# Fourier branch: the position sums made once for both mirrored halves, z gated by one Silu, and a gate group placed first of the eight projection groups

## The chip, the cores and the metric

One Trainium2 chip, one core of it. The metric is the device time of one execution in microseconds (us). It was 1290.96 us before, the median of 3 runs (1290.1 to 1291.08). Everything is float32; each product is made of three matmuls of rounded parts, as shown below.

## The reference, cut to what matters

```python
def _fourier_mix(u):                       # u: (1, 512, 512), four channel groups of 128
    ug = u.reshape(b, n, 4, 128)
    y = jnp.fft.fftn(ug, axes=(1, 3), norm="ortho").real
    return y.reshape(b, n, 512)

def _merge(p_rest, attn, w_pa, w_pb, w_o): # p_rest: columns of h @ w_in
    ...
    g_a = sigmoid(...); g_b = sigmoid(...)                 # 2 x 2048 gate columns
    y_a = (attn * silu(z_a)) @ w_pa
    y_b = (_fourier_mix(u_b) * silu(z_b)) @ w_pb
    return (g_a * y_a + g_b * y_b) @ w_o

# h = modulate(rmsnorm(x)), p = h @ w_in;  q (12 heads) and k are normalised per head and rotated (rope);
# hc = modulate(rmsnorm(ctx)) gives 256 more keys and values;  out = rmsnorm(x + gate * y)
```

512 tokens, 256 context tokens, width 2048, `w_in` has 9216 columns. The transform of a group is 512 points over the tokens by 128 over the channels. With A the transform over the tokens, the result at token frequency k is C·Re A(k) plus or minus S·Im A(k), where C and S are the cosine and sine tables over the 128 channels, and frequency 512-k has the same two sums with the other sign.

## The kernel before, in words

**Three matmuls for one product.** A float32 operand is split in a rounded part "hi" (ScalarE, ACT, L180) and the rest "lo" (VectorE, DVE, L181). A product is hi·hi + hi·lo + lo·hi, three matmuls on TensorE (PE, L338, L339, L340, the function `mm3`). Weights stream from HBM, are split in the same way, and each split buffer is given back when PE has used it, so ACT and DVE run some five pieces ahead of PE and no further.

**The start** (0 to 144 us) makes h and, from the first weight columns, u and z of the Fourier branch. z stands in `part[:, 4:8]`.

**The channel stage** (144.6 to 156.1 us) is the Fourier transform, for channel groups g of 0 to 3. `tokens(g)` makes the transform over the tokens, frequencies 0 to 256, in two accumulators (even and odd frequencies), and splits them into `ah` and `al`. `positions(g)` makes the sums over the channels: before, it makes 512 outputs in one accumulator `pd`, the columns 0 to 255 and the columns 256 to 511 from the mirrored frequencies (a slice with step -1), each with its own matmuls; `fch` holds the split tables cos, -sin and sin. One DVE instruction (L944) scales the result and multiplies it with the gated z. `gate_b(g)` gates z: Sigmoid on ACT (L949) and a product on DVE (L950). PE's order in this stage is written out by hand: tokens 0, tokens 1, positions 0, tokens 2, positions 1, tokens 3, positions 2, positions 3.

**Eight projection groups** (156.1 to about 810 us) follow, each 1024 columns of `w_in` by a fast product of seven block products, `P1, Q5, P2, Q6, P7, Q3, Q4`, four pieces of weights each. A piece is 12 matmuls of 512 columns, so a group has 28 pieces. `KINDS` names what a group yields: "qz" (512 columns of q and 512 of z_a), "gate" (1024 gate columns), "kv". In the first group (g == 0) DVE also makes and splits the sums of h's blocks that all groups use (`make_form`, `split_form`, L993, L994). A group's results come in four blocks: (0,0) after P2, (1,1) after P7, (0,1) after Q3, (1,0) after Q4.

- A gate block: one Sigmoid (L1182) and a store by ACT's DMA queue (L1183).
- A qz block (0,0) or (1,0) is rotated by `rotated`: squares on ACT (L1208), products into the tile `qr` and into a PSUM scratch pair (DVE, L1210 and L1212), the root on GpSimd (POOL, L1196, L1197), the add (L1215) and the scaling (L1216) on DVE, then two stores of 256 KB each from `qr` on ACT's DMA queue (L1230). A block of z_a takes Tanh and one product.
- PSUM pairs with the tag "y" take turns in two slots: Q5's accumulator, the scratch of a rotation and that of a Tanh.

**The context** needs its own norm. `context_squares` (four pieces `cn`) sums squares, `context_norm` makes the root and two diagonal blocks (DVE, L1315) in the first 256 columns of `qr`, `context_spread` spreads the norms over the partitions by two matmuls on PE (L1320), and `context_row` (four pieces `cr`) writes the modulated context into `qr` and stores it to `cf_d`, from where the kv group reads it. `context_piece` sets beside which piece of which group they stand. `qr` is thus shared by the rotations and the context.

**Order.** After the channel stage a scheduler orders the instructions of each engine when the program is built; on the chip each engine runs its list in that order and waits where an operand is late. `jobs` are small steps, one taken behind each piece.

Of the kernel before, what the change touches and what calls it, by code (L numbers as in the profile page):

```python
# [10 lines left out]
F32 = mybir.dt.float32  # L11
F32R = mybir.dt.float32r
# [6 lines left out]
P = 128  # L19
D = 2048  # L20
T = 512
# [26 lines left out]
EVEN = 258  # L48
# [16 lines left out]
KINDS = ("qz", "qz", "qz", "gate", "gate", "kv", "gate", "gate")  # L65
# [57 lines left out]
def block_kernel(ctx, tc, xT, ctx_rows, ctx_toks, x, c_row, w_ss, w_gate, vecs, qkg, rope, dft_c, dft_s,  # L123
# [243 lines left out]
    for p in start_pieces():  # L367
        if p[2:5:2] == (KK - 4, 0):
            stream(("dfts", 0), dft_s[:, : 2 * EVEN], 2 * EVEN, 2, "raw")
            stream(("dftc", 0), dft_c, 3 * P, 1, "raw")  # L370
        elif p[2:5:2] == (KK - 4, 4):
            stream(("dfts", 1), dft_s[:, 2 * EVEN :], T, 2, "raw")
        stream(("start", p), w_start[p[0] : p[0] + P * p[1]].rearrange("(p c) -> p c", p=P), p[1], p[2 + 1])
# [146 lines left out]
    fch = ppool.tile([P, 2, 3 * P], F32R, name="fch")  # L520
    fsq = [ppool.tile([P, 2, 2, EVEN], F32R, name="fsq0")]
# [374 lines left out]
    fsq.append(fnp.tile([P, 2, 2, 256], F32R, name="fsq1"))  # L896
# [21 lines left out]
    def tokens(g):  # L918

        ah, al = (fnp.tile([P, 2, 257], F32R, tag=n, bufs=2, name=uid(n)) for n in ("ah", "al"))  # L920
        c = slice(P * g, P * g + P)
        for e in range(2):
            n = fsq[e].shape[-1]
            acc = bank()
            for a in range(2):
                mm3(acc[:, :n], uh[:, a, e, c], ul[:, a, e, c], fsq[e][:, 0, a, :], fsq[e][:, 1, a, :], a == 0, a == 1)
            k = slice(e, 257 - e, 2)
            low[g] = split_from(acc[:, :n].rearrange("p (r f) -> p r f", r=2), ah[:, :, k], al[:, :, k])[1]
        AH[g] = ah, al

    def positions(g):

        ah, al = AH.pop(g)
        acc = bank2()
        steps = [(256 * q, P * (r and 1 + q), (slice(0, 256) if q == 0 else slice(256, 0, -1)), r)
                 for q in range(2) for r in range(2)]
        for n, (o, t, k, r) in enumerate(steps):
            for m, i in enumerate((0, 1)):
                nc.tensor.matmul(acc[:, o : o + 256], fch[:, i, t : t + P], ah[:, r, k], start=n == m == 0, stop=False,
                                 skip_group_check=True)  # L940
        for n, (o, t, k, r) in enumerate(steps):
            nc.tensor.matmul(acc[:, o : o + 256], fch[:, 0, t : t + P], al[:, r, k], start=False, stop=n == 3,
                             skip_group_check=True)
        nc.vector.scalar_tensor_tensor(part[:, 4 + g, :], acc, 1.0 / 256.0, part[:, 4 + g, :], op0=ALU.mult, op1=ALU.mult)  # L944

    def gate_b(g):
        z = part[:, 4 + g, :]
        e = fnp.tile([P, T], F32, tag="sil", bufs=1, name=uid("e"))
        nc.scalar.activation(e, z, ACT.Sigmoid)  # L949
        nc.vector.tensor_tensor(z, z, e, op=ALU.mult)  # L950
# [269 lines left out]
    def qz_done(half, c, v, t):  # L1220

        if c:
            e = pair("x" if half else "y")
            nc.scalar.activation(e, v, ACT.Tanh, scale=0.5)
            nc.vector.scalar_tensor_tensor(v, e, 1.0, v, op0=ALU.add, op1=ALU.mult)
            r = v.rearrange("p t (h d) -> p t h d", h=4)
        else:
            r = rotated(half, v, pair("y"))
        for b in range(2):
            nc.scalar.dma_start(qz_d[4 * group.g : 4 * group.g + 4, :, c, 2 * half + b, :].rearrange("h p d -> p h d"),  # L1230
                                r[:, b])
# [72 lines left out]
    def context_squares(i, raw):  # L1304

        nc.scalar.activation(raw, raw, ACT.Square, accum_out=sums[:, i : i + 1])

    def context_norm():

        ss = sums[:, 4:6]  # L1310
        nc.vector.tensor_tensor(ss, sums[:, 0:4:2], sums[:, 1:4:2], op=ALU.add)
# [11 lines left out]
    def context_row(i, raw):  # L1323
# [11 lines left out]
        for j in range(2):  # L1335
            sa, sb = (shift[:, 2 * i + j + 8 * q, 1:2] for q in range(2))
            d = sums[:, 6 + j : 7 + j]
# [651 lines left out]
def _constants():  # L1989
# [10 lines left out]
    dft_c = np.concatenate([np.cos(a), -np.sin(a), np.sin(a)], axis=1).astype(np.float32)  # L2000
# [6 lines left out]
    dft_s = np.concatenate([table(np.arange(0, T // 2 + 1, 2)), table(np.arange(1, T // 2, 2))], axis=1)  # L2007
# [3 lines left out]
def _layout(x, c, ctx, c_ctx, w_ada, b_ada, norm_g, w_in, q_norm_g, k_norm_g, w_proj_a, w_proj_b, w_out, final_g):  # L2011
# [36 lines left out]
    d["w_g"] = blocks(np.concatenate(heads + [w_in[:, O_GA:O_GB], w_in[:, O_K:O_ZA], w_in[:, O_GB:]], axis=1))  # L2048
# [20 lines left out]
```

## Time and profile before

| | |
|---|---|
| time, median of 3 runs | 1290.96 us |
| the profiled execution's own time | 1290.61 us |
| its span (first to last instruction) | 1288.8 us |
| granted TensorE clock | 0.998 |
| PE busy | 1272.9 us, 99% of the span |
| DVE busy | 994.7 us, 77% |
| ACT busy | 682.2 us, 53% |
| POOL busy | 170.8 us, 13% |
| read from HBM | 283.36 MB |

Matmuls are pipelined: a matmul of 512 columns is shown with about 390 ns, but the next starts 227 ns after it. Time lost on PE is read from the distance of starts, not from the busy share. Starts and durations are in us from the span's start. "T" below is the start of a projection group on PE. Numbers behind tile names (whi, wlo, wr, s, y, x, pd) are buffer numbers of the build and mean nothing else.

### The profile page before, as it was taken

What the parts mean: (1) busy time and instruction counts of PE and PEld (TensorE: products, weight loads), DVE (VectorE), ACT (ScalarE), POOL (GpSimd) and SP (SyncE); (2) the same over time, 40 slices, a digit from 0 to 9 for tenths busy, and PEclk for the clock granted to TensorE, in tenths of its full rate; (3) what the DMA queues carried; (4) which work ended last, traced back from release to release, by engine and by line L of the source; (5) the groups of instructions that cost most, each with busy time, mean ns of one, the idle gap of its engine ahead of it and who ended that gap; (6) DMA issues with size and microseconds to landing.
All of it is one profiled execution on the core that took longest, in us unless ns stands there. A gap on an engine that the chain in (4) does not pass through costs nothing.

```text
span 1288.8 us, 17680 instructions
## 1 busy us (share of the span) xinstructions
PE 1272.9 (99%) x6586; PEld 1047.9 (81%) x6586; DVE 994.7 (77%) x1305; ACT 682.2 (53%) x1073; POOL 170.8 (13%) x222
## 2 busy tenths in 40 slices
PE   8999999999999999999999999999999999999997
PEld 5677887888888888888888888888888888888886
DVE  5767899889779787658587666788898777887677
ACT  5322654645556555444355544666667646464544
POOL 0000011111102011012031010012100211211210
PEclk9999999999999999999999999999999999999999
DMA  9998588888988988977879897578852989998986
GB/s 378 408 369 344 208 216 248 237 218 261 227 302 236 301 269 260 291 197 184 278 207 259 286 249 237 182 245 241 270 178 75 249 244 258 244 211 229 225 200 179
DMA packets 104486, 319.14 MB, mean 248 GB/s; under 512 B 9904, under 2 KB 33072, under 8 KB 100432
## 3 DMA queue, kind: packets, MB, share of 16 engines
q1 hardware_dynamic: 55056, 197.40, 42.3%
q0 software_dynamic: 27024, 98.19, 35.6%
q10 hardware_dynamic: 22320, 22.42, 5.1%
q8 instruction: 51, 0.84, 0.3%
q14 instruction: 35, 0.29, 0.1%
HBM read 283.36 MB, written 34.61 MB: 247 GB/s over the span
## 4 chain that ended last, share of the span: by engine, by line
PE 91%; DVE 3%; DMA 2%; ACT 2%; issue 1%; SPq 0%; ACTq 0%; DVEq 0%
PE banks L338 10%; PE banks L339 10%; PE banks L340 10%; PE x L340 9%; PE x L338 9%; PE x L339 9%; PE y L340 7%; PE y L339 7%; PE y L338 7%; PE banks L1543 2%; PE pd L566 2%; PE pb L338 1%; PE pb L339 1%; PE pb L340 1%; PE pc L338 1%; DMA wa<-in_w_ss 1%
## 5 line engine op out<-in xcount | busy, mean ns | idle before, releaser
L180 ACT ACTIVATE whi<-R 128x1024 fp32r<-128x1024 f32 x138 | 145.6, 1060 | 142.1 <-PE banks L340 55.3
L181 DVE TENSOR_TENSOR wlo<-R,whi 128x1024 fp32r<-128x1024 f32 x138 | 167.9, 1222 | 57.9 <-ACT whi L180 57.6
L181 DVE TENSOR_TENSOR wlo<-wr,whi 128x1024 fp32r<-128x1024 f32 (+1 forms) x122 | 147.2, 1214 | 63.1 <-ACT whi L180 63.1
L180 ACT ACTIVATE whi<-wr 128x1024 fp32r<-128x1024 f32 (+1 forms) x122 | 127.4, 1052 | 127.3 <-PE y L340 44.3
L338 PE MATMUL banks<-whi,s 128*128 128x512 f32 (+1 forms) x400 | 157.8, 394 | 0.9 <-DVE ev L1106 0.9
L339 PE MATMUL banks<-wlo,s 128*128 128x512 f32 (+1 forms) x400 | 155.8, 389 | 0.0
L340 PE MATMUL banks<-whi,s 128*128 128x512 f32 (+1 forms) x400 | 155.8, 389 | 0.0
L338 PE MATMUL x<-whi,s 128*128 128x512 f32 x352 | 137.1, 390 | 0.0
L340 PE MATMUL x<-whi,s 128*128 128x512 f32 x352 | 137.0, 389 | 0.0
L339 PE MATMUL x<-wlo,s 128*128 128x512 f32 x352 | 136.9, 389 | 0.0
L338 PE MATMUL y<-whi,s 128*128 128x512 f32 x316 | 123.1, 389 | 0.2 <-DVE cxe L1266 0.2
L339 PE MATMUL y<-wlo,s 128*128 128x512 f32 x316 | 123.1, 390 | 0.0
L340 PE MATMUL y<-whi,s 128*128 128x512 f32 x316 | 122.8, 389 | 0.0
L291 POOL DMA_DIRECT2D R<-in_w_g x64 | 56.0, 875 | 415.2 <-DVE wlo L181 212.6
L180 ACT ACTIVATE s<-wr 128x512 fp32r<-128x512 f32 (+2 forms) x93 | 60.9, 678 | 68.1 <-DMA wr<-cf_d 24.9
L338 PEld LDWEIGHTS banks<-whi,s 128*128 128x128 f32 x400 | 75.2, 188 | 16.6 <-DVE ev L1106 1.3
L181 DVE TENSOR_TENSOR s<-wr,s 128x512 fp32r<-128x512 f32 (+2 forms) x93 | 66.7, 750 | 28.3 <-ACT s L180 27.5
L340 PEld LDWEIGHTS banks<-whi,s 128*128 128x128 f32 x400 | 75.1, 188 | 15.3
L339 PEld LDWEIGHTS banks<-wlo,s 128*128 128x128 f32 x400 | 75.2, 188 | 13.6 <-DVE wlo L181 0.2
L340 PEld LDWEIGHTS x<-whi,s 128*128 128x128 f32 x352 | 66.1, 188 | 13.8
L339 PEld LDWEIGHTS x<-wlo,s 128*128 128x128 f32 x352 | 66.1, 188 | 13.7
L338 PEld LDWEIGHTS x<-whi,s 128*128 128x128 f32 x352 | 66.1, 188 | 13.6
(322 smaller groups left out, 2803.2 us busy)
## 6 DMA issues: line engine op xcount, KB each, us to landing
wr<-in_w_g SPq DMA_DIRECT2D x128, 512.0 KB, 5.8
R<-in_w_g POOLq DMA_DIRECT2D x64, 512.0 KB, 7.3
wa<-in_w_ss SPq DMA_DIRECT2D x31, 1024.0 KB, 9.7
R<-in_w_g SPq DMA_DIRECT2D x32, 512.0 KB, 6.0
wr<-in_w_gate SPq DMA_DIRECT2D x32, 512.0 KB, 5.1
wr<-in_w_o SPq DMA_DIRECT2D x24, 512.0 KB, 7.5
R<-in_w_o POOLq DMA_DIRECT2D x24, 512.0 KB, 9.2
wr<-in_w_pab SPq DMA_DIRECT2D x20, 512.0 KB, 6.0
```

The source lines that it names most:

```text
L180: first = nc.scalar.activation(hi, src, ACT.Copy)
L181: return first, nc.vector.tensor_tensor(lo, src, hi.bitcast(F32), op=ALU.subtract)
L291: nc.gpsimd.dma_start(chain[e.pc], e.nxt, accum_op=ALU.add)
L338: nc.tensor.matmul(o, ah, bh, start=start, stop=False, skip_group_check=cont)
L339: nc.tensor.matmul(o, ah, bl, start=False, stop=False, skip_group_check=cont)
L340: nc.tensor.matmul(o, al, bh, start=False, stop=stop, skip_group_check=cont)
L566: nc.tensor.matmul(acc[32 * j : 32 * j + 32], c2[:, n, :], w[:, k, :], start=n < 4, stop=n >= KK - 4)
L1543: nc.tensor.transpose(tp[:, k * P : (k + 1) * P], p[:, k * P : (k + 1) * P], ident)
```

## The change

What it does:

- `positions` makes two sums of 258 columns, C·Re A in the accumulator `pd` and S·Im A in `pc`, by three matmuls each. ACT copies the second to SBUF (`odd`), DVE subtracts (columns 0 to 256) and adds in mirrored order (columns 257 to 511) and multiplies with z. The table of sines loses its second copy, the scale 1/256 goes into the table, and the odd frequencies get one more (257), so that both halves have 258 columns.
- `gate_b` is one Silu on ACT, in place.
- `KINDS` starts with a gate group, the three qz groups come second to fourth, and the columns of `w_g` are laid out to match. The context's squares, norm and rows move with them: squares in the fourth group from P7 on, the norm behind the first piece of the fifth group, the spread two jobs later, and the rows at pieces 5, 10, 15 and 20 of the fifth group.

```diff
-KINDS = ("qz", "qz", "qz", "gate", "gate", "kv", "gate", "gate")
+KINDS = ("gate", "qz", "qz", "qz", "gate", "kv", "gate", "gate")
...
+CTX_NORM, CTX_ROWS = (16, 18, 20, 22), (33, 38, 43, 48)
 def context_piece(g, name, pc):
     n = 28 * (g - NQZ) + 4 * ONE_GROUP.index(name) + pc
-    if n % 2 == 0 and 0 <= n < 8:
-        return "cn", n // 2
-    if n % 7 == 4 and 18 <= n < 46:
-        return "cr", n // 7 - 2
+    if n in CTX_NORM:
+        return "cn", CTX_NORM.index(n)
+    if n in CTX_ROWS:
+        return "cr", CTX_ROWS.index(n)
...
     def tokens(g):
-        ah, al = (fnp.tile([P, 2, 257], F32R, tag=n, bufs=2, name=uid(n)) for n in ("ah", "al"))
+        ah, al = (fnp.tile([P, 2, FREQ], F32R, tag=n, bufs=2, name=uid(n)) for n in ("ah", "al"))
...
     def positions(g):
         ah, al = AH.pop(g)
-        acc = bank2()
-        steps = [(256 * q, P * (r and 1 + q), (slice(0, 256) if q == 0 else slice(256, 0, -1)), r)
-                 for q in range(2) for r in range(2)]
-        for n, (o, t, k, r) in enumerate(steps):
-            for m, i in enumerate((0, 1)):
-                nc.tensor.matmul(acc[:, o : o + 256], fch[:, i, t : t + P], ah[:, r, k], start=n == m == 0, stop=False,
-                                 skip_group_check=True)
-        for n, (o, t, k, r) in enumerate(steps):
-            nc.tensor.matmul(acc[:, o : o + 256], fch[:, 0, t : t + P], al[:, r, k], start=False, stop=n == 3,
-                             skip_group_check=True)
-        nc.vector.scalar_tensor_tensor(part[:, 4 + g, :], acc, 1.0 / 256.0, part[:, 4 + g, :], op0=ALU.mult, op1=ALU.mult)
+        acc = [b()[:, :FREQ] for b in (bank2, bank3)]
+        for r, o in enumerate(acc):
+            t = slice(P * r, P * r + P)
+            mm3(o, fch[:, 0, t], fch[:, 1, t], ah[:, r, :], al[:, r, :], True, True)
+        z = part[:, 4 + g, :]
+        y, odd = (fnp.tile([P, n], F32, tag=t, bufs=2, name=uid(t)) for t, n in (("y", T), ("odd", FREQ)))
+        nc.scalar.copy(odd, acc[1])
+        nc.vector.tensor_tensor(y[:, :257], acc[0][:, :257], odd[:, :257], op=ALU.subtract)
+        nc.vector.tensor_tensor(y[:, 257:], acc[0][:, 255:0:-1], odd[:, 255:0:-1], op=ALU.add)
+        nc.vector.tensor_tensor(z, y, z, op=ALU.mult)

     def gate_b(g):
         z = part[:, 4 + g, :]
-        e = fnp.tile([P, T], F32, tag="sil", bufs=1, name=uid("e"))
-        nc.scalar.activation(e, z, ACT.Sigmoid)
-        nc.vector.tensor_tensor(z, z, e, op=ALU.mult)
+        nc.scalar.activation(z, z, ACT.Silu)
...
     def context_norm():
-        ss = sums[:, 4:6]
+        ss = sums[:, 28:30]
...
     for g, kind in enumerate(KINDS):
-        if g == 3:
-            jobs += [lambda: None] * 12 + [context_norm, lambda: None, lambda: None, context_spread]
+        if g == KV - 1:
+            jobs += [context_norm, lambda: None, context_spread]
...
-    dft_c = np.concatenate([np.cos(a), -np.sin(a), np.sin(a)], axis=1).astype(np.float32)
+    dft_c = (np.concatenate([np.cos(a), np.sin(a)], axis=1) / 256.0).astype(np.float32)
...
-    dft_s = np.concatenate([table(np.arange(0, T // 2 + 1, 2)), table(np.arange(1, T // 2, 2))], axis=1)
+    dft_s = np.concatenate([table(np.arange(e, FREQ, 2)) for e in range(2)], axis=1)
```

The line numbers of the changed kernel are other ones: what is L268, L276, L1106, L1210, L1212, L1215, L1216, L1315, L1320 before is L271, L279, L1105, L1209, L1211, L1214, L1215, L1314, L1319 after.

**PE, channel stage, before:** `positions(0)` and the first product of `tokens(2)`.

```order
L939 MATMUL pd252_1482<-ah243_1439,fch_146 128x256 x8
L942 MATMUL pd252_1482<-al244_1440,fch_146 128x256 x4
L338 MATMUL pb255_1498<-fsq0_147,uh_1346 128x258
L339 MATMUL pb255_1498<-fsq0_147,uh_1346 128x258
L340 MATMUL pb255_1498<-fsq0_147,ul_1347 128x258
```

**PE, the same place, after:**

```order
L341 MATMUL pd251_1480<-ah243_1439,fch_146 128x258
L342 MATMUL pd251_1480<-al244_1440,fch_146 128x258
L343 MATMUL pd251_1480<-ah243_1439,fch_146 128x258
L341 MATMUL pc252_1481<-ah243_1439,fch_146 128x258
L342 MATMUL pc252_1481<-al244_1440,fch_146 128x258
L343 MATMUL pc252_1481<-ah243_1439,fch_146 128x258
L341 MATMUL pb257_1496<-fsq0_147,uh_1346 128x258
```

Twelve matmuls became six, and the first one that reads `al` stands second, where it stood ninth.

**DVE, end of the channel stage, before,** from the last `al` of `tokens(2)` on (`al260` is that of `tokens(3)`).

```order
L181 TENSOR_TENSOR al254_1497<-pb256_1507,ah253_1496 128x2x128
L181 TENSOR_TENSOR wlo268_1575<-R1_1340,whi267_1574 128x1024
L944 SCALAR_TENSOR_TENSOR part_108<-pd258_1519,part_108 128x512
L181 TENSOR_TENSOR al260_1534<-pb261_1535,ah259_1533 128x2x129
L181 TENSOR_TENSOR al260_1534<-pb262_1544,ah259_1533 128x2x128
L181 TENSOR_TENSOR wlo272_1596<-R2_1341,whi271_1595 128x1024
L944 SCALAR_TENSOR_TENSOR part_108<-pd266_1560,part_108 128x512
```

**DVE, the same place, after** (`al264` is that of `tokens(3)`).

```order
L184 TENSOR_TENSOR al256_1495<-pb258_1505,ah255_1494 128x258
L943 TENSOR_TENSOR y261_1523<-pd259_1515,odd262_1524 128x257
L944 TENSOR_TENSOR y261_1523<-pd259_1515,odd262_1524 128x255
L184 TENSOR_TENSOR al264_1530<-pb265_1531,ah263_1529 128x258
L945 TENSOR_TENSOR part_108<-y261_1523,part_108 128x512
L184 TENSOR_TENSOR al264_1530<-pb266_1540,ah263_1529 128x258
L943 TENSOR_TENSOR y271_1562<-pd269_1554,odd272_1563 128x257
L944 TENSOR_TENSOR y271_1562<-pd269_1554,odd272_1563 128x255
L184 TENSOR_TENSOR wlo274_1569<-R1_1340,whi273_1568 128x1024
```

Three DVE rows stand where L944 stood, and the split of the second weight piece (`wlo` from R1) moved behind the last `al`.

**DVE, the diagonal blocks of the context's norm, before** (fourth group, a gate group, among the splits for P7).

```order
L276 TENSOR_TENSOR wr504_3569<-R0_1339,wr504_3569 128x1024
L181 TENSOR_TENSOR s72_434<-R3_1342,s70_433 128x2x256
L1315 TENSOR_SCALAR qr_1617<-ident_86,small_97 128x128 x2
L181 TENSOR_TENSOR s97_572<-wr504_3569,s95_571 128x2x256
L276 TENSOR_TENSOR wr507_3587<-R1_1340,wr507_3587 128x1024
```

**DVE, the same instruction, after** (fifth group, during P1, right behind the last rotation of the fourth group).

```order
L1211 TENSOR_TENSOR y549_3894<-ev504_3488,qr_1609 128x8x32 x2
L184 TENSOR_TENSOR s72_434<-R3_1342,s70_433 128x2x256
L1214 TENSOR_TENSOR qr_1609<-qr_1609,y549_3894 128x1024
L184 TENSOR_TENSOR s97_572<-wr562_4014,s95_571 128x2x256
L1215 TENSOR_TENSOR qr_1609<-qr_1609,small_97 128x1024
L184 TENSOR_TENSOR s128_735<-wr562_4014,s126_734 128x2x256
L1314 TENSOR_SCALAR qr_1609<-ident_86,small_97 128x128 x2
L184 TENSOR_TENSOR wlo566_4061<-wr563_4034,whi565_4060 128x1024
```

The blocks are now written into `qr` one row behind the scaling (L1215), whose result the two stores of 256 KB have to read out of `qr` first.

**PE, the spread of the context's norm, after:** in the second piece of Q5 of the fifth group, 69 matmuls behind the group's start (48 of P1, 21 of Q5).

```order
L341 MATMUL y559_3995<-whi555_3960,s287_1658 128x512
L342 MATMUL y559_3995<-wlo556_3961,s287_1658 128x512
L343 MATMUL y559_3995<-whi555_3960,s288_1659 128x512
L1319 MATMUL y557_3977<-qr_1609,ones_91 128x128 x2
L341 MATMUL y559_3995<-whi555_3960,s287_1658 128x512
```

Before, the same two matmuls stood at the end of Q6 of the fourth group. The accumulator y559 of this Q5 lies in the PSUM slot that held y549, the scratch of the last rotation.

More of the change, by code (lines that the diff above doesn't have):

```diff
@@ L47 @@
 HL, MORE_HL = 3, 2
-EVEN = 258
+FREQ = 258
 FORMS = ("Z5", "S2", "S3", "S4")
@@ L1229, in qz_done @@
         for b in range(2):
-            nc.scalar.dma_start(qz_d[4 * group.g : 4 * group.g + 4, :, c, 2 * half + b, :].rearrange("h p d -> p h d"),
+            nc.scalar.dma_start(qz_d[4 * group.g - 4 : 4 * group.g, :, c, 2 * half + b, :].rearrange("h p d -> p h d"),
                                 r[:, b])
```

30 lines of the change are left out of this document (15 added, 15 removed).

## Prediction, on record before the changed kernel ran

> **What bounds the kernel now.** The first part of the page says it:
>
> ```profile
> PE 1272.9 (99%) x6586; PEld 1047.9 (81%) x6586; DVE 994.7 (77%) x1305; ACT 682.2 (53%) x1073; POOL 170.8 (13%) x222
> PE 91%; DVE 3%; DMA 2%; ACT 2%; issue 1%; SPq 0%; ACTq 0%; DVEq 0%
> ```
>
> The second row, from the chain that ended last, shows that PE is the path nearly everywhere. So a matmul taken away counts in full, and work added to DVE, ACT or a queue counts only where PE then waits for it. Next the windows, one row for the channel stage and one for each of the first five projection groups (length, then PE, PEld, DVE busy):
>
> ```profile
> 144.60:156.10 11.50, 11.50 (x97) 11.50 (x96) 11.22 (x21) 8.48 (x16) 0.53 (x1) 1.00 0.20 79
> 156.10:234.10 78.00, 77.05 (x339) 62.89 (x338) 75.57 (x88) 42.22 (x63) 10.51 (x13) 1.00 0.80 229
> 234.10:310.20 76.10, 76.10 (x337) 63.04 (x336) 66.77 (x80) 40.99 (x77) 11.33 (x12) 1.00 0.89 249
> 310.20:386.40 76.20, 76.20 (x337) 63.07 (x337) 59.41 (x75) 41.80 (x81) 10.76 (x12) 1.00 0.87 251
> 463.00:539.20 76.20, 76.20 (x337) 63.07 (x337) 55.85 (x78) 39.49 (x51) 6.90 (x8) 1.00 0.90 274
> ```
>
> A group costs 76.2 us when PE never waits; the first costs 78.0, with DVE busy 75.6 of them. PE's timeline shows where most of the 1.8 us goes, each time at a form or weight that DVE has split late:
>
> ```profile
> 208.06 0.39 PE L338 MATMUL x<-s,s 128*128 128x512 f32 x1
> 209.16 0.50 PE L339 MATMUL x<-s,s 128*128 128x512 f32 x1 [0.71 <-DVE s L181]
> 212.01 0.39 PE L339 MATMUL y<-s,s 128*128 128x512 f32 x1
> 212.64 0.50 PE L340 MATMUL y<-s,s 128*128 128x512 f32 x1 [0.24 <-DVE s L181]
> ```
>
> Starts 1.10 and 0.63 apart instead of 0.23 (as 386.40 to 386.63 below): 1.3 us lost, plus restarts.
>
> **The channel stage.** Positions before, on PE:
>
> ```profile
> 154.68 1.12 PE L939 MATMUL pd<-ah,fch 128*128 128x256 f32 x8
> 155.64 0.65 PE L942 MATMUL pd<-al,fch 128*128 128x256 f32 x4
> 156.13 0.40 PE L338 MATMUL x<-whi,s 128*128 128x512 f32 x1
> ```
>
> Twelve matmuls from 154.68 to 156.13 are 1.44 us, 0.120 each. The change takes 24 of 48 away: 24 x 0.120 = 2.9 us. The two columns more in each matmul are under 0.1 us together.
>
> What they covered is tight, though. The first matmul on `al` was the ninth, now it is the second. The durations are these:
>
> ```profile
> L180 ACT ACTIVATE ah<-pb x8: 392/409/419, 145.5 to 153.4; 128x258 fp32r<-128x258 f32 x4, 128x256 fp32r<-128x256 f32 x4
> L181 DVE TENSOR_TENSOR al<-pb,ah x8: 417/422/428, 146.4 to 153.9; 128x258 fp32r<-128x258 f32 x4, 128x256 fp32r<-128x256 f32 x4
> 155.36 0.69 DVE L944 SCALAR_TENSOR_TENSOR part<-pd,part 128x512 f32<-128x512 f32 x1
> 145.80 0.69 DVE L950 TENSOR_TENSOR part<-part,e 128x512 f32<-128x512 f32 x1
> 138.43 1.28 ACT L949 ACT_TABLE_LOAD   x1
> ```
>
> Followed through the new order from 144.6 on, tokens 3 ends on PE at 151.8 and positions 3 starts at 152.5. DVE, which has no idle time here, reaches the last `al` at about 153.2 and ends it at 153.5, while PE wants it at 152.6. So about 0.9 us of the gain is given back; the ends are 0 (DVE on time) and 1.4 (one DVE row of 512 later). DVE's own work hardly changes: four L944 and four L950 go (4.8 us at 0.6 from start to start), four rows each of 257, 255 and 512 columns come (5.1 us). No row shows a mirrored read on DVE; L1212 reads swapped halves of 256 columns at 0.43, like `al`, so I take that, with nothing and 0.34 more for each as ends. The `odd` copies are 0.4 each on ACT, idle for 3 of 11.5 us here. Silu has no row; I take Sigmoid's, and nothing on the path follows from it for some 5 us. The gate group first costs one more table load, 1.28 us on ACT, idle for 36 us in that group: nothing. Net of the stage: -2.0 us.
>
> **The first group.** As a gate group it loses the first rotation's DVE rows that stood before 208 us:
>
> ```profile
> L1210 DVE TENSOR_TENSOR qr<-x,qr x8: 683/688/692, 193.6 to 592.6; 128x512 f32<-128x512 f32 x8
> L1212 DVE TENSOR_TENSOR y<-x,qr x12: 422/427/433, 194.2 to 353.9; 128x256 f32<-128x256 f32 x12
> L1216 DVE TENSOR_TENSOR qr<-qr,small x8: 1217/1220/1226, 202.7 to 670.0; 128x1024 f32<-128x1024 f32 x8
> ```
>
> Two L1210, four L1212, an L1215 and an L1216: by starts 2 x 0.6 + 4 x 0.33 + 2 x 1.13 = 4.8 us. PE arrives 2.0 earlier and had waited 1.8, together 3.8; DVE is 4.8 - 1.3 (the new waits inside the channel stage) = 3.5 earlier. It nearly breaks even: I let 0.4 us of waits stay, so -1.4 us. Ends: -1.8 and 0.
>
> **The context's norm behind the last rotation.** This is new, and PE waits for it. The fourth group is now a qz group; its last rotation falls into P1 of the fifth. Two things hang on it: Q5 takes the PSUM slot of the rotation's scratch, free when the add (L1215 before) ends; and the spread's diagonal blocks go into `qr`, free when the first store of the rotation has landed. Where these stood for the three qz groups before, with the start of the next group on PE first:
>
> ```profile
> 234.08 0.39 PE L338 MATMUL x<-whi,s 128*128 128x512 f32 x1
> 246.50 1.22 DVE L1215 TENSOR_TENSOR qr<-qr,y 128x1024 f32<-128x1024 f32 x1
> L1230 ACTq DMA_DIRECT2D qz_d<-qr x2: 366/692/1017, 249.1 to 249.5; - x2
> DMA to landing us min/median/max: 4.7/5.5/6.3
> ...
> 310.24 0.39 PE L338 MATMUL x<-whi,s 128*128 128x512 f32 x1
> 319.54 1.22 DVE L1215 TENSOR_TENSOR qr<-qr,y 128x1024 f32<-128x1024 f32 x1
> L1230 ACTq DMA_DIRECT2D qz_d<-qr x2: 366/443/520, 323.1 to 323.5; - x2
> DMA to landing us min/median/max: 8.6/8.8/9.0
> ...
> 386.40 0.39 PE L338 MATMUL x<-s 128*128 128x512 f32 x1
> 386.63 0.39 PE L339 MATMUL x<-s,s 128*128 128x512 f32 x1
> 400.07 1.22 DVE L1215 TENSOR_TENSOR qr<-qr,y 128x1024 f32<-128x1024 f32 x1
> L1230 ACTq DMA_DIRECT2D qz_d<-qr x2: 367/528/688, 403.6 to 404.0; - x2
> DMA to landing us min/median/max: 11.8/13.1/14.3
> ```
>
> The add ends at T+13.6, T+10.4 and T+14.8, the first store is issued at T+15.0, T+12.9 and T+17.2 and lands (the "min") 4.7, 8.6 and 11.8 us later. None of this cost anything, because nobody needed `qr` or the slot soon. Now PE does: Q5 starts at T + 48 x 0.2267 = T+10.9, the spread at T + 69 x 0.2267 = T+15.65.
>
> By the new order, with these durations: DVE takes the subtraction of (1,0) at about T+1.6, and the splits between the rotation's rows have to wait for weight buffers that PE frees a piece at a time; the third piece's, at T+8.2, sets the last squares on ACT (end T+9.8) and the last L1212 (T+10.5). The add ends at T+12.3, POOL's root too (2.3 us), the scaling at T+14.0. Q5 waits 1.4 us (0 to 3.9 by the three rows). The store is issued at T+14.0. Three or four other transfers are under way then, as in the first two cases, so I take 6 us to land, between 4.7 and 8.6. The blocks take 0.6 more: the spread at T+20.6, 5.0 us late in all, Q5's wait included. Ends: 1.4 (see the quick store below) and 14 (third case: 17.2 + 11.8 + 0.6 - 15.65). DVE is stopped behind the same store, but pieces up to the first of P2 are split ahead, 9 us of PE's work, so nothing is added.
>
> The row that shows the opposite is the store of a rotation in mid-group:
>
> ```profile
> DMA to landing us min/median/max: 2.4/2.6/2.8
> ```
>
> [...]
>
> **The rest.** The context's rows add DVE work of about 8 us to the fifth group, which has 20 idle. The kv group's read of `cf_d` now comes some 25 us later, near the group's start; ends 0 and 4 us, I take 0.
>
> **Sum**, against the profiled execution (span 1288.8, its own time 1290.61, which is 0.35 below the median): -2.0 - 1.4 + 5.0 = +1.6 us. On the median: 1290.96 + 1.6 = 1292.6 us. 0.2%, 2.6 us, is what a measurement of this kernel can tell from no change; this is inside.
>
> **Rivals.**
> - *The store lands late* (the other side): as in the second and third case, 8.6 to 11.8 us, PE stands at the spread until T+23 to T+30, 7.5 to 14 us late: +4 to +10.6, 1295 to 1301.5. It decides from a landing of 7 us on. For it: two of three rows. Against: DVE, stopped at the blocks, frees no raw buffers, so fewer loads can follow the store. 0.28.
> - *The store lands in its quick time,* 2.4 to 2.6 us: the spread would be ready at T+17.0, which Q5's wait of 1.4 covers: -2.0, 1289. [...] Against: all three rows at a group's start. 0.14.
> - *No wait there at all:* the rotation ends earlier (the fourth group has DVE to spare, and T+10.4 was seen once), and the first group gains all: -2.9 to -4.7, 1286.3 to 1288.1. 0.17.
> - *The first group's waits stay* because PE's lead of 2 us meets a DVE that is as late as before: +1.4 on the forecast, 1294. 0.04.
>
> **How the numbers follow.** Forecast, landing 3.5 to 7 us, 1290 to 1293.6: 0.37. Faster: the third rival, with a little of the quick store, 0.19. Same: forecast and most of the quick store, 0.47. Slower: the first and the last rival and the forecast's edge, 0.34. The range for 8 in 10 leaves out half of the third rival and the late end of the first: 1287.5 to 1299.
>
> **What would show it.** Right: 24 matmuls in `pd` and `pc`; a PE wait of about 1 us for `al` before positions 3; the first group at 76.2 to 77; the fifth at 80 to 83, with a wait before Q5's first matmul and one before L1319, the blocks (L1314) held by the store. Wrong: the fifth group at 76.6 or below (no wait), or above 84 (late landing); the first group still at 78; a kv group over what it had.

## The result, and the profile after

The changed kernel took 1300.58 us (median of 5 runs, 1299.31 to 1301.76) against 1290.96; the ratio is 1.0076, with a 95% interval of 1.0062 to 1.009. The forecast was 1292.6, its range up to 1299.0. The profiled execution took 1299.31 us, 1.3 below its median, with a span of 1297.5: 8.7 more than before.

First the page's busy times, then the windows of the stage, the first, fourth and fifth group and the kv group (which has 504 matmuls of 512 columns, where the others have 336), and of before's fourth and kv group for comparison (length, then PE, PEld, DVE, ACT, POOL busy, clock, DMA share, GB/s):

```profile
PE 1271.7 (98%) x6562; PEld 1045.4 (81%) x6562; DVE 996.0 (77%) x1308; ACT 685.2 (53%) x1077; POOL 167.6 (13%) x222
```

```profile
144.60:155.00 10.40, 9.14 (x74) 8.74 (x72) 9.07 (x20) 7.02 (x17) 0.53 (x1) 1.00 0.11 41
155.00:232.20 77.20, 76.80 (x337) 63.02 (x338) 73.48 (x85) 43.78 (x51) 8.57 (x11) 1.00 0.81 242
384.50:460.70 76.20, 76.20 (x338) 63.12 (x337) 62.32 (x75) 44.55 (x84) 12.34 (x14) 1.00 0.86 253
460.70:545.30 84.60, 78.98 (x341) 64.39 (x340) 62.52 (x103) 43.09 (x72) 8.90 (x10) 0.98 0.80 237
545.30:661.40 116.10, 114.75 (x505) 94.38 (x504) 80.20 (x91) 44.20 (x71) 10.61 (x13) 1.00 0.83 251
```

```profile
386.40:463.00 76.60, 76.60 (x341) 63.50 (x340) 65.24 (x93) 43.44 (x72) 11.65 (x12) 1.00 0.91 273
539.20:654.00 114.80, 114.59 (x505) 94.48 (x504) 76.59 (x87) 43.12 (x68) 10.62 (x13) 1.00 0.80 226
```

The stage is 1.1 us shorter (11.5 before), the first group 0.8 (78.0), the fourth 0.5 (76.6: the spread of the context's norm stood there); up to the fifth group the changed kernel is 2.4 us ahead. The fifth group is 8.5 longer, and 0.5 of that is the spread itself, which it now has. In the kv group PE is idle for 1.35 us, where it was for 0.2. Something is lost later too: PE's waits, longest first, from 144 us to the end (the second figure is how often; a wait counts from the modelled end of the matmul ahead, so the loss from start to start is 0.1 to 0.2 more):

```profile
PE y L1319 <- DVE qr L1314: 3.8, 1, 3.8
PE y L342 <- DVE wlo L184: 1.7, 2, 1.3
PE y L341 <- ACT ev L1267: 1.3, 1, 1.3
PE banks L341 <- DVE ev L1105: 0.9, 1, 0.9
PE pd L342 <- DVE al L184: 0.8, 1, 0.8
PE banks L1656 <- DMA s<-yb_d: 0.7, 1, 0.7
PE y L341 <- DVE qr L1214: 0.5, 1, 0.5
PE banks L341 <- DVE R L1490: 0.5, 1, 0.5
PE x L341 <- ACT odd L942: 0.5, 1, 0.5
```

L1105 (0.9) stood before too. New are the two of the channel stage (al, odd), one at 172 us in the first group (the smaller L184, 0.4), four in the fifth group and the kv group (L1214, L1314, the longer L184, L1267), and two late ones (R L1490 at 909 us, s<-yb_d at 1131). In sum: stage -1.1, first group -0.8, fourth -0.5, fifth +8.5, kv +1.25, seventh and eighth -0.2, the rest +1.5, together the 8.7. The medians differ by 9.6; the profiled execution is the fastest of the five, and what the others lose more is on no trace.

**The fifth group** starts on PE at T = 460.65. The rotation's last rows on DVE, its store on ACT's queue with the time to landing, and PE at the spread:

```profile
472.61 1.21 DVE L1215 TENSOR_TENSOR qr<-qr,small 128x1024 f32<-128x1024 f32 x1
...
480.63 0.48 DVE L1314 TENSOR_SCALAR qr<-ident,small 128x128 f32<-128x128 f32 x2 [6.21 <-DMA qz_d<-qr]
```

```profile
L1229 ACTq DMA_DIRECT2D qz_d<-qr x2: 366/634/903, 473.9 to 474.3; - x2
DMA to landing us min/median/max: 6.7/6.9/7.0
```

```profile
481.07 0.68 PE L1319 MATMUL y<-qr,ones 128*128 128x128 f32 x4 [3.81 <-DVE qr L1314]
...
482.35 0.63 PE L341 MATMUL y<-whi,s 128*128 128x512 f32 x1
482.78 0.63 PE L342 MATMUL y<-wlo,s 128*128 128x512 f32 x1
...
485.34 0.53 PE L342 MATMUL y<-wlo,s 128*128 128x512 f32 x1
485.71 0.39 PE L343 MATMUL y<-whi,s 128*128 128x512 f32 x1
```

```profile
482.30:485.60 3.30, 3.30 (x9) 2.57 (x8) 3.30 (x8) 1.75 (x3) 0.00 (x0) 0.50 0.61 170
```

The store is issued at T+13.2, lands 6.7 us later, the blocks follow at once, the spread at T+20.4. Then comes something that the prediction has no term for: the matmuls behind the wait start 0.427 us apart in place of 0.227, at a granted clock of 0.50, for 3.3 us. The eight from 482.35 to 485.71 lose 1.5 us together.

What goes with such a stretch at half clock is taken up in the last section.

**Later in the group**, ACT at a split of weights; the fourth context row on DVE, ahead of a split that PE wants; SP's queue around the first load of the finished context, what SP waited for there, and the same load in the kernel before; ACT at a later one:

```profile
521.47 1.06 ACT L183 ACTIVATE whi<-wr 128x1024 fp32r<-128x1024 f32 x1 [6.02 <-DMA wr<-in_w_g]
```

```profile
526.92 1.67 DVE L1330 SCALAR_TENSOR_TENSOR qr<-wr,gain,qr 128x256 f32<-128x256 f32 x4 [0.73 <-DMA cf_d<-qr]
...
530.55 1.22 DVE L184 TENSOR_TENSOR wlo<-wr,whi 128x1024 fp32r<-128x1024 f32 x1
```

```profile
532.93 0.33 SPq L222 DMA_DIRECT2D R<-in_w_g  x1
535.61 0.38 SPq L219 DMA_DIRECT2D wr<-cf_d  x1
```

```profile
SPq L222 <- DVE wlo L184: 17.3, 4, 14.9
```

```profile
SPq L219 <- DMA cf_d<-qr: 2.3, 1, 2.3
```

```profile
509.15 0.39 SPq L216 DMA_DIRECT2D wr<-cf_d  x1
```

```profile
563.29 0.63 ACT L183 ACTIVATE s<-wr 128x512 fp32r<-128x512 f32 x1 [4.46 <-DMA wr<-cf_d]
```

ACT stands 6.0 us for a weight until 521.5, and DVE, which splits behind it, 5.0. The row then waits 0.7 us until the third row's store has left qr, and the split at 530.55 stands behind the row: PE loses 1.4 us at 530. Which of the two weighs more, the late weight or the row, this trace doesn't tell. The first load of cf_d left SP at 509 us before; now it leaves at 535.6. Ahead of it stood a weight load that waited 15 us for its buffer (the longest of that row), and then 2.3 us for the last row's store, issued at 531.8 and 3.8 us on its way. In the kv group ACT stands at a piece of cf_d until 563.3, with the copy that PE needs (L1267) behind it: 1.5 us.

### The profile page after: what moved, and what is told of

Read it like the earlier page. It is cut to its first block, busy times and chain, and to the rows that moved or that the text cites. A ratio compares the mean times of both kernels' runs of the same rounds, so it can differ in the third digit from the quotient of the medians.

```text
span 1297.5 us, 17647 instructions
## 1 busy us (share of the span) xinstructions
PE 1271.7 (98%) x6562; PEld 1045.4 (81%) x6562; DVE 996.0 (77%) x1308; ACT 685.2 (53%) x1077; POOL 167.6 (13%) x222
## 4 chain that ended last, share of the span: by engine, by line
PE 51%; ACT 2%; DVE 1%; DMA 1%; issue 1%; ACTq 0%
PE banks L341 10%; PE banks L342 9%; PE banks L343 9%; PE y L341 3%; PE y L342 3%; PE y L343 3%; PE x L342 3%; PE x L343 3%; PE x L341 3%; PE banks L1542 2%; DMA s<-yb_d 1%; PE banks L1656 1%; DMA wr<-in_w_pab 0%; PE banks L1557 0%; ACT s L1526 0%
## 5 line engine op out<-in xcount | busy, mean ns | idle before, releaser
L184 DVE TENSOR_TENSOR wlo<-R,whi 128x1024 fp32r<-128x1024 f32 x138 | 168.0, 1221 | 57.4 <-ACT whi L183 56.9
L184 DVE TENSOR_TENSOR wlo<-wr,whi 128x1024 fp32r<-128x1024 f32 (+1 forms) x123 | 148.0, 1211 | 61.6 <-ACT whi L183 61.5
L341 PE MATMUL y<-whi,s 128*128 128x512 f32 x320 | 125.7, 393 | 1.9 <-ACT ev L1267 1.3
L343 PE MATMUL y<-whi,s 128*128 128x512 f32 x320 | 125.0, 391 | 0.0
L184 DVE TENSOR_TENSOR s<-wr,s 128x512 fp32r<-128x512 f32 (+2 forms) x91 | 65.8, 749 | 30.0 <-ACT s L183 29.2
```

The costliest lines, as they stand in the source:

```text
L184: return first, nc.vector.tensor_tensor(lo, src, hi.bitcast(F32), op=ALU.subtract)
L341: nc.tensor.matmul(o, ah, bh, start=start, stop=False, skip_group_check=cont)
L343: nc.tensor.matmul(o, al, bh, start=False, stop=stop, skip_group_check=cont)
```

## The experiments

Each time below is a median and stands beside runs of the kernel before (1290.73 to 1291.18) on the same chip, with the ratio to those. The intervals reach 1 to 2 us to each side; where a mechanism is smaller, its wait is read from the trace.

**The blocks in other columns.**

```diff
-    crs, diag = qr[:, 1792:], qr[:, :256]...
+    crs, diag = qr[:, 1792:], qr[:, 1792:]...
```

> The changed kernel with one edit: the diagonal blocks of the context's norm go into columns 1792 to 2047 of qr (those that the spread's own result takes afterwards), which no store reads, so they need not wait for the landing of qz_d<-qr. Theory A (the fifth group's loss is this wait, the slow clock behind it, and two later waits that the late context rows cause): the wait of 4.1 us at L1319, the nine matmuls at half clock behind it (1.6 us) and 0.4 of restarts go, 1300.6 - 6.1 = 1294.5; if the rows then also come earlier, the waits of 1.4 at the fourth row and 1.5 in the kv group go as well, 1291.5. Rival B (the store still decides: the first context row's DVE work, L1330, now waits for it, and with it the splits behind it): PE stands some 4 us later in the fifth group instead, no gain over 2 us, 1298.5 or more.

Measured: 1296.97, ratio 1.0049 (1.0036 to 1.0061); 3.6 us of the 9.6 come back, between the two expectations. The wait at L1319 and the half clock are gone, so both hung on the store. But DVE now meets the same store at the first context row, ACT waits for a weight about as long as in the changed kernel (6.0 us there), and PE, which is now earlier, waits too:

```profile
480.41 0.88 DVE L1330 SCALAR_TENSOR_TENSOR qr<-wr,gain,qr 128x256 f32<-128x256 f32 x2 [5.71 <-DMA qz_d<-qr]
```

```profile
518.50 1.06 ACT L183 ACTIVATE whi<-wr 128x1024 fp32r<-128x1024 f32 x1 [5.82 <-DMA wr<-in_w_g]
```

```profile
PE y L342 <- DVE wlo L184: 3.3, 3, 2.3
```

```profile
460.40:542.40 82.00, 78.13 (x342) 63.24 (x340) 62.07 (x104) 42.59 (x72) 9.34 (x10) 1.00 0.82 244
```

The fifth group is 82.0 us, 2.7 less: 5.7 taken away, 3 of it back at 513 to 529 us. A context row that waits for a store stops DVE and keeps a raw weight buffer; that this is why the weights come late is read from the queues, not shown by a run.

**The rows closer together.**

```diff
-CTX_ROWS = (33, 38, 43, 48)
+CTX_ROWS = (33, 37, 41, 45)
```

> The changed kernel with CTX_ROWS = (33, 37, 41, 45) in place of (33, 38, 43, 48): the last context row eight us earlier, the spread's wait untouched. Theory A (the 1.5 us in the kv group is the load of cf_d, which stands on SP's queue behind the last row's store, and the 1.4 us in the fifth group is the fourth row's DVE work ahead of a split): both go, 1300.6 - 2.9 = 1297.7, with the wait at L1319 still 4 us and the matmuls behind it at half clock. Rival B (those waits come from loads that run late for another reason, since the DMA engines are 80 to 90% busy there): same time within 1 us, 1299.6 to 1301.6, or slower by up to 2 us, since four pieces of 2.7 us leave less time for each store of a row to land before the next row overwrites it.

Measured: 1301.03, 1.008 (1.0066 to 1.0094). The time is rival B's, but both waits that theory A names are gone. A wait of 2.8 at 519 us has come in the fifth group instead, with a second stretch at half clock behind it:

```profile
PE x L342 <- DVE s L184: 2.8, 1, 2.8
```

```profile
520.50:523.00 2.50, 2.50 (x7) 1.94 (x6) 2.35 (x4) 1.06 (x1) 0.00 (x0) 0.50 1.06 218
```

Neither spacing of the four rows fits between the rotation's store and the load of cf_d: closer, the second row waits 3.7 us for the first one's store, and DVE stands 4.7 us at 516 for a late weight, which is what PE waits for; wider, kv waits. That the closer rows make the weight late is not shown.

**The stage alone** (sums once, Silu, tables; order and context as before).

```diff
-KINDS = ("gate", "qz", "qz", "qz", "gate", "kv", "gate", "gate")
+KINDS = ("qz", "qz", "qz", "gate", "gate", "kv", "gate", "gate")
...
```

> The kernel before with the channel stage's part of the change alone (sums once, Silu, new tables), the order of groups and the context as before. Theory A (the stage gives 1.1 us on PE: 24 matmuls, 2.9, less a wait of 1.0 for al and one of 0.7 for the odd copy; the first group as a qz group then hands it back, because PE arrives earlier at forms that DVE splits late): stage 1.1 shorter, waits near 208 and 212 us larger by up to 1.1, 1289.9 to 1291. Rival B (DVE leaves the stage later than before, by its own waits, and the qz group pays for it): first group over 79.5 us, 1291.5 or more.

Measured: 1293.6, 1.002 (1.0011 to 1.0028): slower, rival B. The stage itself is 1.1 us shorter, but the first group, a qz group here, takes 81.8 in place of 78.0:

```profile
154.80:236.60 81.80, 78.08 (x337) 62.77 (x338) 78.70 (x93) 44.49 (x65) 10.48 (x13) 1.00 0.79 223
```

DVE's four splits of wr, which before had at 207.81, start here at 210.26, and PE comes 1.4 us earlier. The two rows, first this kernel's, then before's:

```profile
210.26 2.50 DVE L184 TENSOR_TENSOR s<-wr,s 128x512 fp32r<-128x512 f32 x4
```

```profile
207.81 2.50 DVE L181 TENSOR_TENSOR s<-wr,s 128x512 fp32r<-128x512 f32 x4
```

**The order alone** (`tokens`, `positions`, `gate_b` and the tables of before in the changed kernel).

```diff
-        nc.scalar.activation(z, z, ACT.Silu)
+        e = fnp.tile([P, T], F32, tag="sil", bufs=1, name=uid("e"))
+        nc.scalar.activation(e, z, ACT.Sigmoid)
+        nc.vector.tensor_tensor(z, z, e, op=ALU.mult)
...
```

> The changed kernel with the channel stage of before: gate group first and the context moved, nothing else. Theory A (the loss is the order's, the parts add up): first group 0.8 to 1.8 us shorter than before's 78.0, the fifth group 8 us longer with the store's wait of 4 us at L1319, kv and the rest 1 to 3 us longer, 1291 + 8.5 + 1.3 + 0 to 1.5 - 0.8 to 1.8 - 0.5 = 1299 to 1302. Rival B (without the new stage the first group gains nothing, since it was the stage's shorter DVE work that let it): first group at 78 still, 1301 to 1303.

Measured: 1303.38, 1.0095 (1.0081 to 1.0109). The time is over both ranges. Theory A in kind (the first group is 76.7 us), but the kv group's wait is 4.2 and the Q5 wait 1.2, both larger than in the changed kernel (the spread's, second, is 3.4):

```profile
PE y L341 <- ACT ev L1271: 4.2, 1, 4.2
PE y L1323 <- DVE qr L1318: 3.4, 1, 3.4
```

The parts don't add up: alone +2.9 and +12.7, together +9.6. In front of a qz group the new stage and the first group take 2.7 us longer together than with the old stage (92.2 and 89.5), in front of a gate group 0.6 less (87.6 and 88.2). That is a part of the difference only: the fifth and the kv group take 86.2 and 121.0 us here, 84.7 and 116.1 in the changed kernel, and why, no run shows.

**kv one group later, the context spaced as before.**

```diff
-KINDS = ("gate", "qz", "qz", "qz", "gate", "kv", "gate", "gate")
+KINDS = ("gate", "qz", "qz", "qz", "gate", "gate", "kv", "gate")
...
-CTX_NORM, CTX_ROWS = (16, 18, 20, 22), (33, 38, 43, 48)
+CTX_NORM, CTX_ROWS = (28, 30, 32, 34), (46, 53, 60, 67)
...
```

> The changed kernel with KINDS = (gate, qz, qz, qz, gate, gate, kv, gate) and the context's steps set as far behind the last qz group as in the kernel before (squares from the start of the fifth group, norm twelve jobs later, rows seven pieces apart in the fifth and sixth groups, kv seventh). Theory A (all of the loss in the fifth and sixth groups is the context squeezed into one group behind the last rotation): no wait over 0.5 us between 460 us and the attention, stage 1.1 and first group 0.8 shorter stay, late waits of 0.5 to 1.5 us behind 900 us stay: 1290.8 - 1.9 + 0 to 1.5 = 1288.9 to 1290.4. Rival B (the kv group one group later leaves too little time for the keys before the attention): a new wait of 1 to 4 us between 690 and 860 us, 1291.5 to 1295.

Measured: 1312.03, 1.0159 (1.0145 to 1.0173): far off, neither. The fifth group has no wait any more, as theory A says; the sixth takes 88.1 us, some 12 more than without waits, and nearly as much is lost behind 698 us:

```profile
460.40:536.60 76.20, 76.20 (x339) 63.15 (x339) 59.60 (x85) 40.51 (x69) 9.08 (x10) 1.00 0.85 248
536.70:624.70 88.00, 80.53 (x337) 63.61 (x336) 65.62 (x96) 38.16 (x52) 7.39 (x9) 0.98 0.94 291
```

The pools of raw and split weight buffers change at steps tied to the kv group, and PE's longest wait in this run, 4.5 us, is for a weight that ACT split late; that was not followed further. It shows that the fifth group is free once the context isn't squeezed behind the rotation; it is no better version.

**The same, with the sine's sum first.**

```diff
-        for r, o in enumerate(acc):
+        for r in (1, 0):
```

> The same with positions making the sum with the sine first, so that ACT copies it while PE makes the other one. Theory A (PE's wait of 0.67 us at the first group's first matmul is the copy odd, which holds the PSUM bank): the copy starts 0.36 earlier, the wait falls to about 0.3, the time by 0.3 to 0.4 us, to 1288.6 to 1290.1; too little to be told by the times, so it is read from the wait. Rival B (something else is late there too, or DVE's subtraction then holds the other bank): the first group starts within 0.15 us of where it did.

Measured: 1312.87 (1.0164), not to be told from the one above. The wait is read on PE: the first group starts 0.43 behind the last sum, 0.31 over the pace, where it was 0.79 (154.20 to 154.99), 0.67 over it. Theory A: PE waits for the copy that frees the bank.

```profile
154.70 0.28 PE L343 MATMUL pd<-ah,fch 128*128 128x258 f32 x1
155.13 0.50 PE L341 MATMUL x<-whi,s 128*128 128x512 f32 x1
```

**The stage alone with the table of channel sums as large as before** (a third block that nothing reads).

```diff
-    fch = ppool.tile([P, 2, 2 * P], F32R, name="fch")
+    fch = ppool.tile([P, 2, 3 * P], F32R, name="fch")
...
-    dft_c = (np.concatenate([np.cos(a), np.sin(a)], axis=1) / 256.0)...
+    dft_c = (np.concatenate([np.cos(a), np.sin(a), np.sin(a)], axis=1) / 256.0)...
```

> The stage alone (order of before) with the table of channel sums as large as before, in HBM and in SBUF: a third block that nothing reads. The order of the instructions behind the stage is that of the stage alone. Theory A (the late waits, 0.4 us at R L1490 near 903 and 1.2 at s<-yb_d near 1125 us, which all kernels with the new stage show and those with the old one don't, come from where the tensors lie): they go, 1293.6 - 1.6 = 1292.0. Rival B (they come from the other phase between loads and PE, or from tables of other sizes than this one): they stay, 1293 to 1294.

Measured: 1293.88, 1.0025 (1.0016 to 1.0033). Rival B: the late waits stay (s<-yb_d 0.9, R L1490 0.3).

**The stage alone with the product with z on POOL.**

```diff
-        nc.vector.tensor_tensor(z, y, z, op=ALU.mult)
+        nc.gpsimd.tensor_tensor(z, y, z, op=ALU.mult)
```

> The stage alone (order of before) with the product with z on POOL in place of DVE, four rows of 512 columns. Theory A (the stage alone is slower because DVE leaves the stage later and a qz group, whose forms DVE splits just in time, is behind it): DVE has 4 x 0.6 = 2.4 us less to do, the first group's waits fall from 4.9 us to 2.5 to 3.4, 1293.6 - 1.5 to 2.4 = 1291.2 to 1292.1. Rival B (DVE is not what is late; ACT, or the weights' loads, are): waits and time as with DVE, 1293 to 1294, or more if POOL's rows hold up the branch.

Measured: 1293.6, 1.0019 (1.001 to 1.0028). Theory A by the late splits, rival B by the time. In the first group the late splits cost 1.7 us in place of 4.9, more than theory A asked, and the group takes 79.8 us in place of 81.8; but the stage takes 11.5 in place of 10.4: the wait for al grew from 0.8 to 1.8, and POOL's rows are slow, 1.3 to 2.3 us each. Behind that wait the clock granted was 0.50 again, from 155.2 to 158.7, and five of the first group's matmuls start 0.427 apart, which is 1.0 us of its time (the two windows are shown in the last section).

```profile
L945 POOL TENSOR_TENSOR part<-y,part x4: 1277/1707/2271, 150.4 to 157.2; 128x512 f32<-128x512 f32 x4
```

**The stage alone, the first rotation put off by ten steps; the kernel before with the same; and the first with the sine's sum first.**

```diff
+            elif name == "P2" and self.g == 0:
+                after(10, lambda: self.done(0, 0, a, None))
             elif name == "P2":
                 self.done(0, 0, a, None)
```

> The stage alone (order of before) with the first group's first rotation put off by ten steps, so that its DVE rows (two L1209, four L1211, L1214, L1215, 4.8 us) stand behind the forms of h that PE needs near 208 to 214 us. Theory A (the stage is slower in front of a qz group because these rows and the stage's own delay DVE's forms; nothing else of the order matters): the first group's waits fall from 4.9 us to under 1, 1293.6 - 4 = 1289.6. Rival B (the rotation is then late itself, and its PSUM pair or the stores hold up the second group): waits of 1 us or more behind 221 us, 1291.5 or more.

> The kernel before with the same ten steps and nothing else. Theory A (the first group's 1.3 us of waits at 208 and 212 us hang on the rotation's rows): they go, 1290.8 - 1.3 = 1289.5. Rival B (the forms are late for ACT or the weights, not for DVE's rows): the waits stay within 0.3 us, 1290.5 to 1291.

> The stage alone with the rotation put off and the sine's sum first. Theory A: as with the rotation put off, and PE's wait for odd 0.31 in place of 0.67 as in the run with the kv group later: 0.3 us less, 1289.3. Rival B (the gain of the stage is spent in the first group whatever is put off): over 1290.5.

Measured: 1290.18 (0.9992, 0.9984 to 1.0001), 1289.08 (0.9989, 0.998 to 0.9998) and 1289.82 (0.9992, 0.9983 to 1.0001). Theory A three times by the first group: it is 77.2, 76.8 and 77.3 us (the first two below), and the waits at 208 to 214 are gone in all three:

```profile
155.20:232.40 77.20, 76.83 (x337) 62.99 (x338) 75.98 (x91) 43.78 (x65) 10.42 (x13) 1.00 0.79 226
```

```profile
156.40:233.20 76.80, 76.49 (x339) 63.05 (x338) 74.96 (x87) 42.00 (x63) 10.42 (x13) 1.00 0.84 227
```

The two kernels with the new stage lose 1.3 us in the second group (a split of DVE near 288, a sign of rival B, though not for its reason) and more at the late waits, and the new stage gives nothing beyond that. The kernel before with the rotation put off has the lowest time of all, 1.4 us under before by the ratio, and of the three it alone has an interval that leaves out no change; from the other two it isn't to be told.

**The kernel before with the position table as long as in the changed one.**

```diff
...
-    dft_s = np.concatenate([..., table(np.arange(1, T // 2, 2))], axis=1)
+    dft_s = np.concatenate([..., table(np.arange(1, T // 2, 2)), table(np.arange(1, 3, 2))], axis=1)
```

> The kernel before with the position table in HBM as long as in the changed kernel (4 columns more that nothing reads); every engine's instructions are the same. Theory A (the late waits of the kernels with the new stage, 0.4 to 1.2 us at R L1490 and 0.5 to 1.5 us at s<-yb_d, come from where the tensors lie in HBM): they appear here, at R L1491 near 900 and s<-yb_d near 1124 us, and the time is 1291.5 to 1292.5. Rival B (they come from the instructions or the phase): no such wait, 1290.8.

Measured: 1290.9, 1.0 (0.9991 to 1.001), no late wait. Rival B.

**Program code moved.** All ten kernels so far with the new stage wait for s<-yb_d, by 0.15 to 1.3 us, none of the four with the old one. PE's order is the same there. What differs is when a packet of program code comes (queue q8, which the profile calls instruction; one packet of 16 KB). Windows of one us, the changed kernel at 1126.4, 5 us ahead of PE's need (1131.4), and the kernel before at 1113.5, 10 us ahead of its need (1123.8); packets, MB, share of 16 engines:

```profile
q8 instruction: 1, 0.02, 8.7%
```

```profile
q8 instruction: 1, 0.02, 6.1%
```

8.7% of 16 engines' us is 1.4 us on one engine, 6.1% is 1.0. With the new stage the packet falls 3 to 5 us ahead of the need, while that load is under way; with the old one 9 to 12 us ahead, at its start or before. PE has 24 matmuls and as many weight loads less (6562 and 6586), at its pace of 0.2267 us an estimated 24 x 0.2267 = 5.4 us of its program. To test it, 24 came back at the start:

```diff
         warm(8, ones)
+        warm(12, ones[:, :4])
```

> The stage alone with the rotation put off, the sine's sum first, and twelve float32 matmuls of 4 columns (24 PE instructions) behind the eight that stand at the program's start, where PE then idles for 2 us. Theory A (the load s<-yb_d lands late because a packet of program code for PE is moved in the middle of it, since 24 matmuls fewer stand ahead): the packet is moved 10 to 12 us before PE needs the load again, the wait of 0.85 us goes, 1289.8 - 0.9 = 1288.9. Rival B (the code is a bystander): the packet moves back, the wait stays, 1289.8.

> The changed kernel with the same twelve matmuls of 4 columns at the start. Theory A: the waits of 0.86 us at s<-yb_d and perhaps of 0.68 at R L1490 go, 1300.6 - 0.9 to 1.5 = 1299.1 to 1299.7. Rival B: they stay, 1300.6.

Measured: 1290.77 (0.9998, 0.9989 to 1.0007) and 1301.78 (1.0081, 1.0068 to 1.0095). In both the packet is back at 10 to 12 us ahead of the need and the wait for s<-yb_d is gone; in the second the one for R L1490 too. In all sixteen kernels the place of the packet and the wait go together: 3.4 to 4.8 us ahead with the wait (ten), 9.8 to 11.6 without (six). That is theory A for the cause, though the twelve matmuls also move PE against the loads, and no run moves the packet alone. The times did not gain. The twelve matmuls were not free: PE is 2.7 us later at the stage (its first group starts at 157.3 in place of 154.6). The second run also lost 1.3 us more in the fifth group and 3.0 in the kv group than the changed kernel, which was not followed.

## Why the prediction was wrong, point by point

- **The channel stage, -2.0: measured -1.1.** The 24 matmuls went, and the wait for al cost 0.97 from start to start (0.9 said). Mis-sized by a wait that was not in the sum: the step "the odd copies are 0.4 each on ACT, idle" looked at ACT's load and not at the bank that the last copy holds, which P1's accumulator takes next. 0.67 us, cut to 0.31 by the other order of sums.
- **The first group, -1.4: measured -0.8.** The direction holds: the rotation's rows are what PE waits for at 208 and 212 (they were put off in the kernel before, and the waits went). The 0.4 us of waits that was left to stay is 0.57 at 172 us, but not at a form of h: it is a late split of a weight. It differs from run to run (0 to 0.6 in the seven kernels with a gate group first, whose first groups take 76.7 to 77.4 us; 0.5 in the run with the longer position table, which has the instructions of before), so it can't be put down to the change.
- **The fifth group, +5.0: measured +8.0,** and 0.5 for the spread, which only moved there from the fourth. The chain was right nearly to the number: store issued at T+13.2 (14.0 said), landing 6.7 us (6), spread at T+20.4 (20.6), Q5's wait 0.7 (1.4). The 2.4 to 2.8 us in which the rotation's store issued at 358.3 us, in mid-group, landed before did not come back at this place: 6.7 was measured. What makes one landing quick and another slow was not shown. What failed is the step from the wait to its price: "nothing is added" behind the 5.0 us. Behind it came 1.5 us at half clock. And the context's rows, put at nothing since DVE "has 20 idle", came with a wait of 1.4 at the fourth row: not all of DVE's idle time was room for them, since 5.0 us of it lay at a late weight just ahead. The rival of a late landing gave 1295 to 1301.5 and so held the time, but not for this reason, so that was luck: the landing was of the forecast's 3.5 to 7 us.
- **"The rest", 0: measured +1.25 in the kv group and +1.5 behind.** The first lies within the ends given (0 to 4 us) and was taken at 0; it went when the rows were put closer together. The second goes with the place of the code packet; the prediction has no term for what fewer instructions do to the rest of the program.
- **The chances.** Slower was given 0.34. The misses of the sum all lie on that side: the stage by 0.9, the first group by 0.6, the fifth by 3.0, the kv group and what is behind it by 2.6.

The stage and the gate group first were right together: the stage alone costs 2.9 us because DVE comes out of it late and meets the rotation. What made the kernel slower is in the main where that puts the context, one group between the last rotation and kv, with one tile for both: with the blocks in other columns 3.6 us came back, with closer rows the kv group's 1.25, and with the context a group later the fifth group had no wait. None of the three beat the kernel before, since other waits took the place, and no run puts the gate group first without losing time around the context.

## What to carry to other kernels

A tile shared by two tenants is free only when the first one's store has landed (here 6.7 us after its issue); when a reorder moves them together, price the landing by the slowest row of that place, and then the half clock that came behind the wait (here 1.5 us behind 3.8) and the next wait in line: with the first one taken away, PE met the next. A stage made shorter gains nothing if an engine leaves it late and the next stage needs that engine first (alone, the shorter stage cost 2.9 us here): look there for a row that can be put off, which here gave no less than the stage and the same row put off together. With 24 matmuls less on PE at 145 to 155 us, a packet of program code came some 5 us ahead of PE's need for a load at 1131 us, in place of 10 in the kernel before, and PE waited 0.7 us there; a wait that appears far behind an edit may be of this kind.

## What the runs showed of the hardware that was not expected

- **Half clock behind a wait.** Of PE's waits behind 144 us, each of the ten whose starts were 2.8 to 4.9 us apart, in six kernels, had 5 to 13 matmuls at half clock behind it (1 to 2.6 us more); two of 2.59 and 2.64 had none, two of 2.15 and 2.31 had 5 and 6. So the length of a wait doesn't decide alone. In these sixteen traces what tells is how much of a stretch PE is busy, by the profile's modelled ends. The records of the granted clock in the trace of the changed kernel last 3.413 us or, within 0.08 us, a multiple of it, save the last one at the program's end; the only one at 0.50 behind 144 us and ahead of that end runs from 482.22 to 485.63, and PE was busy for 1.15 us of the 3.41 ahead of it. On that grid, behind 144 us (the program's last 20 us left out), each of the 13 stretches at full clock in which PE was busy for 1.6 us or less had half clock behind it, while none with 1.67 or more had. This is read from the traces; no run was made to test it. The wait of 2.15, by POOL, lay in one stretch and the clock fell; the wait of 2.59, with the order alone, was parted by a border and it did not:

```profile
151.82:155.23 3.41, 1.59 (x11) 1.20 (x9) 3.41 (x6) 0.67 (x2) 1.75 (x3) 1.00 0.29 113
155.24:158.65 3.41, 2.90 (x8) 2.32 (x8) 3.41 (x5) 3.22 (x4) 3.41 (x2) 0.50 0.11 43
```

```profile
530.07:533.48 3.41, 1.67 (x8) 1.05 (x6) 3.38 (x10) 2.18 (x5) 0.00 (x0) 1.00 0.12 47
533.48:536.89 3.41, 2.95 (x13) 2.41 (x14) 1.62 (x3) 1.52 (x3) 0.00 (x0) 1.00 0.72 269
```

- **A packet of program code of 16 KB took one DMA engine 1.0 us in the kernel before and 1.4 in the changed one** (6.1% and 8.7% of 16 engines' us). Where it came in the middle of a load that PE needed soon, PE waited 0.15 to 1.3 us (the ten kernels above); that the load waits for the one engine that has the packet is argued, not shown.
- **POOL's product of 512 columns** took 1.3 to 2.3 us beside DVE's 0.69.
